# A second tile for the sums of the 1024-feature norms, their statistics traced at top priority, and a reciprocal square root by Ln and Exp in the GLA head norms

## The chip, the cores and the metric

The kernel runs on one core of one Trainium2 chip. The metric is the device time of one execution in microseconds; the time before is the median of three runs. A profile is one further execution of the same program, read by the hardware profiler. Its engines are TensorE (PE in the rows, with its weight loads as PEld), VectorE (DVE), ScalarE (ACT), GpSimd (POOL) and SyncE (SP, which here only issues transfers).

## What is computed

One inference step of a two-layer hybrid backbone over 640 tokens: 128 context tokens and 512 latent tokens, 1024 features each. Layer 0 mixes tokens by a chunked gated linear attention (GLA, four heads of 128 output features) and a multi-head latent attention side by side; layer 1 does differential attention. Each layer ends in a gated MLP of width 2816 with a width-3 convolution. Ahead of each of these four sublayers, and once more at the end, stands an RMS norm over the 1024 features. The GLA heads have a norm of their own.

```python
def rmsnorm(x, g):
    y = xf * lax.rsqrt(jnp.mean(xf * xf, axis=-1, keepdims=True) + EPS)
    return y * g
def modulate(h, shift, scale):
    return h * (1.0 + scale) + shift
...
hp = modulate(rmsnorm(xp, norm_gain[l, 0]), mp[0], mp[1])     # five norms of this width in all
...
o = rmsnorm(o, gla_gain) * jax.nn.silu(ga)                    # GLA: over the 128 features of a head
```

The shift, scale and gate of each sublayer come from a linear map of the SiLU of a conditioning vector.

## The kernel before

Features lie on the 128 partitions, in eight blocks k of 128 features (`x[:, k]`), and tokens along the free dimension. The 640 tokens are worked in two halves of 320 columns (`CH`). Each projection is a set of matmuls in a split precision: a weight tile and an activation tile each have a high part and a low part, and three matmuls of 128x128 by 320 columns make one product; the high parts are casts on ScalarE, the low parts subtractions on VectorE or GpSimd. `B` holds the normed activations in the two parts, and the matmuls of a sublayer walk over its eight blocks k.

The code is traced by a tile framework, whose planner lays out every engine's queue by a simulated timeline before the kernel runs: of the instructions that are ready there, the one traced earliest goes first, and a tile is taken from its pool's ring when its first writer is laid out. After that each engine works through its queue strictly in order. `tc.issue_after(ins)` keeps what a block traces behind `ins` in the queue of the engine of `ins`; it puts nothing on instructions of other engines. In the code before, `Ada.step` nests one such block for a VectorE instruction and one for a transfer.

The norm over 1024 features is `rms` (L227). For one half it squares block 0 on ScalarE into the tile `racc` (L235), squares blocks 1 to 7 into the two tiles `rsq` (L238), and adds each to `racc` on VectorE (L239). A matmul with a matrix of minus ones sums over partitions and spreads the sum (L242, tile `rb`). ScalarE takes Ln (L244) and Exp (L245, written back into `racc`) for a first value of the reciprocal root, squares it (L247), and two VectorE instructions improve it (L248, L250). `racc` has one buffer, so the half that comes second can begin its first square only when L250 of the first half has read that buffer.

`norm_mod` (L321) is this and then `apply_norm` (L303): for each block k, VectorE multiplies `x` by the spread root and the gain (L311, in two pieces where context and latent tokens meet in the first half), ScalarE adds the shift and makes the high part (L313, L177), and VectorE (L315, even k) or GpSimd (L178, odd k) makes the low part. `norm_mod` runs three times for two halves each: ahead of the MLP of layer 0 (about 430 to 470 us of the profile), ahead of layer 1's attention (about 900 to 945 us), ahead of the MLP of layer 1 (about 1305 to 1340 us). Each time the matmuls of an output projection (`out_mm`, tile `pot`, L345) finish half 0 of `x` first and half 1 after, with a residual addition for each block (L327), so half 0 is normed beside the matmuls of half 1. Then the first matmuls of the next sublayer (`up` at L201, or `qko` and `vo` at L216 and L1051) run over half 0 and after that over half 1.

At the start of the kernel both halves are normed from the loaded `x` (L444) beside the four steps `ada0` (L417), which make shift and scale of the first norm on TensorE, each ended by a copy to SBUF on VectorE (L431); blocks 0 to 3 are modulated after the second of them, blocks 4 to 7 after the fourth. There too ScalarE applies Silu to the gate vectors `cbc` (L471), for use in products on VectorE later (L368). The last norm is `final` (L1179): half 0 is finished on GpSimd (L1187, L1188), half 1 on VectorE (L1190) and stored.

The GLA head norms use `rms_stats` (L253): squares (L260), small matmuls that bring the sums of 64 tokens into columns (L266), and then, on a tile of 64 rows by 8, a reciprocal square root on VectorE alone: a seed from two integer operations (L272, L273) and three Newton steps of three instructions (L275 to L277). The GLA works through five chunks of 128 tokens; it calls `stats` for chunks 0 to 2 in its main loop and for chunks 3 and 4 later, beside the first work of the latent attention. The same function serves the differential attention of layer 1.

Of the kernel before, what the change touches and what calls it, by code (L numbers as in the profile page):

```python
# [7 lines left out]
FP32 = mybir.dt.float32  # L8
# [4 lines left out]
I32 = mybir.dt.int32  # L13
ACTF = mybir.ActivationFunctionType
# [5 lines left out]
D = 1024  # L20
# [36 lines left out]
def build(tc, a):  # L57
# [166 lines left out]
        with tc.issue_after(after.ins) if after else ExitStack():  # L224
            mark["tab"] = S.preload_act_table_set("natural_log_exp_and_others")

    def rms(tp, bank, parts, denom, out=None, y=None, after=None):  # L227

        n = parts[0].shape[-1]

        def sq_tile():
            return tp.tile([128, CUT], FP32, tag="rsq", name="rsq", bufs=2)[:, 0:n]

        acc = tp.tile([128, CUT], FP32, tag="racc", name="racc")[:, 0:n]
        S.activation(out=acc, in_=parts[0], func=ACTF.Square)  # L235
        for s in parts[1:]:
            sq = sq_tile()
            S.activation(out=sq, in_=s, func=ACTF.Square)  # L238
            V.tensor_tensor(out=acc, in0=acc, in1=sq, op=ALU.add)  # L239
        o, q, y = bank[:, 0:n], sq_tile(), acc if y is None else y  # L240
        with tc.issue_after(after.ins) if after else ExitStack():
            PE.matmul(out=o, lhsT=negs, rhs=acc, start=True, stop=True)  # L242
        with tc.issue_after(mark["tab"].ins):
            S.activation(out=q, in_=o, func=ACTF.Ln, scale=-1.0 / denom, bias=epst[:, 0:1])  # L244
            S.activation(out=y, in_=q, func=ACTF.Exp, scale=-0.5, bias=lnh[:, 0:1])  # L245
        y = y.bitcast(FP32)
        S.activation(out=q, in_=y, func=ACTF.Square, scale=2.0 / math.sqrt(denom))  # L247
        V.scalar_tensor_tensor(out=o, in0=o, scalar=-denom * EPS, in1=q, op0=ALU.add, op1=ALU.mult)  # L248
        out = o if out is None else out
        V.scalar_tensor_tensor(out=out, in0=o, scalar=3.0, in1=y, op0=ALU.add, op1=ALU.mult)  # L250
        return out

    def rms_stats(tp, bank, srcs, denom):  # L253
        sizes = [s[0].shape[-1] // 64 for s in srcs]
        nb = sum(sizes)
        sums = bank[0:64, 0:2 * nb].rearrange("p (c t) -> p c t", t=2)
        b0 = 0
        for parts, n in zip(srcs, sizes):
            acc = tp.tile([128, CUT], FP32, tag="racc", name="racc")[:, 0:64 * n]
            S.activation(out=acc, in_=parts[0], func=ACTF.Square)  # L260
            for s in parts[1:]:
                sq = tp.tile([128, CUT], FP32, tag="rsq", name="rsq", bufs=2)[:, 0:64 * n]
                S.activation(out=sq, in_=s, func=ACTF.Square)
                mark["acc"] = V.tensor_tensor(out=acc, in0=acc, in1=sq, op=ALU.add)
            for c in range(n):
                PE.matmul(out=sums[:, b0 + c], lhsT=acc[:, c * 64:(c + 1) * 64], rhs=negs[:, 0:2], start=True, stop=True)  # L266
            b0 += n
        y = tp.tile([64, 20], FP32, tag="ry", name="ry")[:, 0:nb]
        v = tp.tile([64, 20], FP32, tag="rv", name="rv")[:, 0:nb]
        t = tp.tile([64, 20], FP32, tag="rt", name="rt")[:, 0:nb]  # L270
        V.tensor_scalar(out=v, in0=sums[:, :, 0], scalar1=-1.0 / denom, scalar2=EPS, op0=ALU.mult, op1=ALU.add)
        V.tensor_scalar(out=t.bitcast(I32), in0=v.bitcast(I32), scalar1=1, scalar2=None, op0=ALU.logical_shift_right)  # L272
        V.tensor_scalar(out=y.bitcast(I32), in0=t.bitcast(I32), scalar1=-1, scalar2=0x5F3759DF, op0=ALU.mult, op1=ALU.add)  # L273
        for _ in range(3):
            V.tensor_tensor(out=t, in0=y, in1=y, op=ALU.mult)  # L275
            V.scalar_tensor_tensor(out=t, in0=t, scalar=-0.5, in1=v, op0=ALU.mult, op1=ALU.mult)
            V.scalar_tensor_tensor(out=y, in0=t, scalar=1.5, in1=y, op0=ALU.add, op1=ALU.mult)  # L277
        return y
# [41 lines left out]

    def norm_mod(tp, bank, x, hl, l, n, half):  # L321
        c0, c1 = CH[half]
        return apply_norm(tp, x, rms(tp, bank, [x[:, k, c0:c1] for k in range(KT)], D), hl, l, n, half)

    def resid(x, k, ps_ap, l, g, c0=0, c1=TOK):
        for s0, s1, c in seg(c0, c1):
# [114 lines left out]
            make_g(0, 0, (g // 2) * 4, (g // 2) * 4 + 4)  # L441

    ada0(0)
    bcs = [rms(xp, ps("s", "rb")[:, 0:512], [x[:, k, c0:c1] for k in range(KT)], D) for c0, c1 in CH]  # L444
    for g in range(1, 4):
        ada0(g)
        if g % 2:
# [20 lines left out]
    adp.after = [last, load]  # L468
    with tc.issue_after(load.ins):
        adp.load(a["cbc"])  # L470
    S.activation(out=adp.cbc, in_=adp.cbc, func=ACTF.Silu)  # L471
    cbd = drp.tile([128, 2, D], FP32, name="cbd")
    nc.gpsimd.dma_start(out=cbd, in_=adp.cbc)
    for c in range(2):
# [228 lines left out]
            S.copy(out=oo[r], in_=op[:, r, 0:256])  # L703

    def stats(c):
        RY[c] = rms_stats(scp, ps("m", "rb"), [[z] for z in OO[c]], 128.0)

    def finish(c):
        oo, y, t0 = OO.pop(c), RY.pop(c), c * 128
# [398 lines left out]
    def diff_after(h, g, q0, n, ops):  # L1108
# [4 lines left out]
        if g == (1 if h == 7 else 2):  # L1113
# [4 lines left out]
                split(o, A[0][:, h], A[1][:, h])  # L1118

            def stats():  # L1120
                y = rms_stats(oo_, ps("p1", "rb"), [[o[:, c0:c1]] for c0, c1 in CH], 128.0)
                later(DLY if h == 6 else 0, lambda: finish(y))

            def later(n, f):
# [54 lines left out]
    def final(c):  # L1179
        c0, c1 = CH[c]  # L1180
        bcs = nm.tile([128, CUT], FP32, tag="bcs", name="bcs") if c == 0 else None
        bc = rms(nm, ps("p1", "rb"), [x[:, k, c0:c1] for k in range(KT)], D, bcs)
        k0 = 0
        for k in range(KT):
            xk, fg = x[:, k, c0:c1], sm["fgain"][:, k:k + 1]
# [174 lines left out]
```

## Time and profile before

| | us |
|---|---|
| median of 3 runs | 1810.37 |
| lowest and highest | 1806.56, 1814.55 |
| the profiled execution | 1809.02 |
| its span, first to last instruction | 1807.2 |

Busy time in that span: TensorE 1740.0 us (96%), VectorE 1263.0 us (70%), ScalarE 759.9 us (42%), GpSimd 312.0 us (17%). The mean granted clock of TensorE is 0.984 of full speed. To read it: TensorE is near to always busy, so what a stage can gain is first the sum of TensorE's pauses there, and then what its clock loses after a pause. Which instruction ended a pause is read from the waits; what that instruction itself stood behind is read from the timelines of the other engines.

### The profile page before, as it was taken

The numbers are of one execution on the slowest core, as the hardware profiler recorded it, in microseconds if no ns is written. First come the engines' busy times: TensorE is split into PE (matmuls) and PEld (weight loads), VectorE is DVE, ScalarE is ACT, GpSimd is POOL, SyncE is SP. The second block draws the span as 40 slices with busy tenths as digits, with TensorE's granted clock in tenths as the row PEclk, the third lists the DMA queues.
The fourth block names the chain that finished last, engine by engine and source line by source line (L and its number), as shares of the span: only waits on it lengthen the run. The fifth ranks groups of instructions, "written<-read, shape, count | busy, mean of one in ns | idle before, by whom it ended". The sixth has DMA issues, their size and how long they took to land. (4 is left out here: it accounts for less than half of the span.)

```text
span 1807.2 us, 29445 instructions
## 1 busy us (share of the span) xinstructions
PE 1740.0 (96%) x11716; PEld 1628.6 (90%) x11716; DVE 1263.0 (70%) x2438; ACT 759.9 (42%) x1344; POOL 312.0 (17%) x330
## 2 busy tenths in 40 slices
PE   7999989999999999999999999999999999999996
PEld 1898777889899999999988999898989999999996
DVE  4964886768699999955588777876575454545556
ACT  5354434544522222322366665665373232323232
POOL 3201021000310100000124233431041010101004
PEclk9999999999999999999999999998999999999998
DMA  9650002035256555522232110211122222222221
GB/s 356 208 177 9 29 1 71 6 141 163 81 170 199 169 186 172 177 61 83 73 116 72 33 58 32 76 49 71 59 72 87 76 71 82 71 82 70 59 83 59
DMA packets 57337, 176.59 MB, mean 98 GB/s; under 512 B 6064, under 2 KB 11568, under 8 KB 56816
## 3 DMA queue, kind: packets, MB, share of 16 engines
q1 hardware_dynamic: 53408, 160.59, 27.8%
q0 software_dynamic: 3792, 14.13, 2.2%
q8 instruction: 92, 1.51, 0.3%
q14 instruction: 45, 0.37, 0.1%
HBM read 166.59 MB, written 7.77 MB: 96 GB/s over the span
## 5 line engine op out<-in xcount | busy, mean ns | idle before, releaser
L207 PE MATMUL up<-B,whi 128*128 128x320 f32 x2560 | 479.2, 309 | 0.0
L163 ACT CAST whi<-wraw 128x1024 fp32r<-128x1024 f32 (+2 forms) x208 | 208.3, 1002 | 505.9 <-PE up L207 231.3
L207 PEld LDWEIGHTS up<-B,whi 128*128 128x128 f32 x2560 | 401.7, 188 | 0.0
L170 DVE TENSOR_TENSOR wlo<-wraw,whi 128x1024 fp32r<-128x1024 f32 (+2 forms) x175 | 205.0, 1172 | 226.2 <-ACT whi L163 226.0
L207 PE MATMUL up<-B,wlo 128*128 128x320 f32 x1280 | 291.5, 309 | 0.0
L207 PE MATMUL po<-A,whi 128*128 128x320 f32 x1312 | 246.2, 309 | 0.7 <-DVE u L972 0.5
L207 PEld LDWEIGHTS up<-B,wlo 128*128 128x128 f32 x1280 | 213.9, 188 | 0.0
L368 DVE CUSTOM_DVE_ANT_0 junk<-araw,cbc 128x1024 bf16<-128x1024 f32 x160 | 203.3, 1271 | 11.1 <-DMA araw<-in_wada0b 8.8
L207 PEld LDWEIGHTS po<-A,whi 128*128 128x128 f32 x1312 | 205.7, 188 | 1.4 <-issue 0.7
L178 POOL TENSOR_TENSOR A<-u,A 128x640 fp32r<-128x640 f32 x44 | 75.8, 1723 | 757.2 <-ACT A L177 732.2
L207 PE MATMUL po<-A,wlo 128*128 128x320 f32 x656 | 149.7, 309 | 0.5 <-DVE wlo L170 0.5
L216 PE MATMUL qko<-B,whi 128*128 128x320 f32 x512 | 119.1, 317 | 2.9 <-ACT B L177 1.5
L170 POOL TENSOR_TENSOR wlo<-wraw,whi 128x256 fp32r<-128x256 f32 (+1 forms) x117 | 97.8, 865 | 134.5 <-ACT whi L163 133.8
L345 PE MATMUL pot<-A,whi 128*128 128x320 f32 x512 | 113.9, 311 | 0.0
L207 PEld LDWEIGHTS po<-A,wlo 128*128 128x128 f32 x656 | 109.6, 188 | 0.8 <-DVE wlo L170 0.8
L970 DVE SCALAR_TENSOR_TENSOR u<-up,small,u 128x127 f32<-128x127 f32 (+1 forms) x176 | 95.4, 542 | 9.0 <-ACT u L968 8.2
L972 DVE SCALAR_TENSOR_TENSOR u<-up,small,u 128x127 f32<-128x127 f32 (+1 forms) x176 | 96.1, 547 | 4.5
L857 ACT ACTIVATE p<-sc,mn 128x768 f32<-128x768 f32 (+1 forms) x100 | 79.2, 796 | 31.9 <-DVE mn L856 31.2
L216 PEld LDWEIGHTS qko<-B,whi 128*128 128x128 f32 x512 | 86.7, 191 | 5.8 <-ACT B L177 2.1
L856 DVE TENSOR_REDUCE mn<-sc 128x1 f32<-128x768 f32 (+1 forms) x100 | 79.2, 815 | 14.6 <-PE sc L831 14.2
L345 PEld LDWEIGHTS pot<-A,whi 128*128 128x128 f32 x512 | 85.7, 188 | 1.1 <-issue 0.4
L207 PE MATMUL pe<-B,whi 128*128 128x320 f32 x416 | 81.5, 318 | 3.1 <-DVE nm_t L311 2.1
(294 smaller groups left out, 3035.4 us busy)
## 6 DMA issues: line engine op xcount, KB each, us to landing
wraw<-in_wup SPq DMA_DIRECT2D x88, 512.0 KB, 3.6
araw<-in_wada SPq DMA_DIRECT2D x48, 512.0 KB, 3.5
wraw<-in_wdn SPq DMA_DIRECT2D x40, 512.0 KB, 3.6
araw<-in_wada0b SPq DMA_DIRECT2D x32, 512.0 KB, 4.3
wraw<-in_wie SPq DMA_DIRECT2D x13, 512.0 KB, 4.4
aw<-in_wada0a SPq DMA_DIRECT2D x8, 512.0 KB, 8.1
wraw<-in_wada0a SPq DMA_DIRECT2D x8, 512.0 KB, 8.0
wraw<-in_woe SPq DMA_DIRECT2D x8, 512.0 KB, 4.3
```

The lines of the kernel that those rows point to most:

```text
L163: S.copy(out=hi, in_=raw)
L170: eng.tensor_tensor(out=lo[:, z], in0=raw[:, z], in1=hi[:, z].bitcast(FP32), op=ALU.subtract)
L178: return (lo_eng or V).tensor_tensor(out=lo, in0=src, in1=hi.bitcast(FP32), op=ALU.subtract)
L207: PE.matmul(out=o, lhsT=w[wi][:, k], rhs=hl[ri][:, k, c0:c1], start=k == 0 and n == 0, stop=k == nk - 1 and n == 2)
L216: PE.matmul(out=o, lhsT=w[wi][:, k], rhs=hl[ri][:, k, c0:c1], start=k == 0 and n == 0, stop=k == nk - 1 and n == 2)
L345: PE.matmul(out=o, lhsT=ws[j + m][wi][:, k], rhs=hl[ri][:, k, c0:c1], start=k == 0 and n == 0, stop=k == nk - 1 and n == 2)
L368: V.tensor_tensor_reduce(out=junk, in0=raw, in1=self.cbc[:, j], op0=ALU.mult, op1=ALU.add, scale=1.0, scalar=0.0, accum_out=mods[l][:, t0 ...
L856: V.tensor_reduce(out=mn[:, m:m + 1], in_=ss[m][:, 0:nk], op=ALU.min, axis=AX.X)
L857: self.exp = S.activation(out=p[:, m, 0:nk], in_=ss[m][:, 0:nk], func=ACTF.Exp, scale=-1.0, bias=mn[:, m:m + 1], accum_out=li[:, m:m + 1])
L970: V.scalar_tensor_tensor(out=u[:, s0 + 1:s1], in0=r[:, s0:s1 - 1], scalar=cw[:, 0:1], in1=u[:, s0 + 1:s1], op0=ALU.mult, op1=ALU.add)
L972: last = V.scalar_tensor_tensor(out=u[:, s0:s1 - 1], in0=r[:, s0 + 1:s1], scalar=cw[:, 2:3], in1=u[:, s0:s1 - 1], op0=ALU.mult, op1=ALU.add)
```

## The change

- `rms` takes the number of buffers of `racc`; the start norm, `norm_mod` and `final` pass 2. The calls with 128 and 256 features keep one.
- In `norm_mod` the call of `rms` is traced inside `tc.high_priority()`, which gives its instructions the priority of the program's start.
- The Silu of `cbc` is traced inside `tc.issue_after(last.ins)`. `last` is what `apply_norm` returned, the VectorE instruction of L315.
- `rms_stats` has a parameter `seed`. Where it is true (the GLA head norms) the two integer operations are replaced by Ln and Exp on ScalarE, queued behind the table load `mark["tab"]`, and one Newton step is made instead of three. The differential attention passes false and stays as it was.

```diff
-    def rms(tp, bank, parts, denom, out=None, y=None, after=None):
+    def rms(tp, bank, parts, denom, out=None, y=None, after=None, bufs=1):
...
-        acc = tp.tile([128, CUT], FP32, tag="racc", name="racc")[:, 0:n]
+        acc = tp.tile([128, CUT], FP32, tag="racc", name="racc", bufs=bufs)[:, 0:n]
...
-    def rms_stats(tp, bank, srcs, denom):
+    def rms_stats(tp, bank, srcs, denom, seed):
...
-        V.tensor_scalar(out=t.bitcast(I32), in0=v.bitcast(I32), scalar1=1, scalar2=None, op0=ALU.logical_shift_right)
-        V.tensor_scalar(out=y.bitcast(I32), in0=t.bitcast(I32), scalar1=-1, scalar2=0x5F3759DF, op0=ALU.mult, op1=ALU.add)
-        for _ in range(3):
+        if seed:
+            with tc.issue_after(mark["tab"].ins):
+                S.activation(out=t, in_=v, func=ACTF.Ln)
+                S.activation(out=y, in_=t, func=ACTF.Exp, scale=-0.5)
+        else:
+            V.tensor_scalar(out=t.bitcast(I32), in0=v.bitcast(I32), scalar1=1, scalar2=None, op0=ALU.logical_shift_right)
+            V.tensor_scalar(out=y.bitcast(I32), in0=t.bitcast(I32), scalar1=-1, scalar2=0x5F3759DF, op0=ALU.mult, op1=ALU.add)
+        for _ in range(1 if seed else 3):
...
     def norm_mod(tp, bank, x, hl, l, n, half):
         c0, c1 = CH[half]
-        return apply_norm(tp, x, rms(tp, bank, [x[:, k, c0:c1] for k in range(KT)], D), hl, l, n, half)
+        with tc.high_priority():
+            bc = rms(tp, bank, [x[:, k, c0:c1] for k in range(KT)], D, bufs=2)
+        return apply_norm(tp, x, bc, hl, l, n, half)
...
-    bcs = [rms(xp, ps("s", "rb")[:, 0:512], [x[:, k, c0:c1] for k in range(KT)], D) for c0, c1 in CH]
+    bcs = [rms(xp, ps("s", "rb")[:, 0:512], [x[:, k, c0:c1] for k in range(KT)], D, bufs=2) for c0, c1 in CH]
...
-    S.activation(out=adp.cbc, in_=adp.cbc, func=ACTF.Silu)
+    with tc.issue_after(last.ins):
+        S.activation(out=adp.cbc, in_=adp.cbc, func=ACTF.Silu)
...
-        RY[c] = rms_stats(scp, ps("m", "rb"), [[z] for z in OO[c]], 128.0)
+        RY[c] = rms_stats(scp, ps("m", "rb"), [[z] for z in OO[c]], 128.0, True)
...
-        bc = rms(nm, ps("p1", "rb"), [x[:, k, c0:c1] for k in range(KT)], D, bcs)
+        bc = rms(nm, ps("p1", "rb"), [x[:, k, c0:c1] for k in range(KT)], D, bcs, bufs=2)
```

## Rows read from the trace of the kernel before

**Rows 1.** The page: its head, and the first line of its part on busy time (busy us, share of the span, instructions).

```profile
span 1807.2 us, 29445 instructions
...
PE 1740.0 (96%) x11716; PEld 1628.6 (90%) x11716; DVE 1263.0 (70%) x2438; ACT 759.9 (42%) x1344; POOL 312.0 (17%) x330
```

**Rows 2.** The waits of TensorE over the whole span: its instruction, the engine and line that ended the pause, the pauses' sum in us, their number, the longest.

```profile
PE up L201 <- ACT B L313: 6.3, 2, 3.2
...
PE rb L242 <- DVE racc L239: 4.2, 1, 4.2
...
PE pe L207 <- DVE nm_t L311: 2.1, 1, 2.1
...
PE up L201 <- DVE B L315: 1.9, 2, 1.0
...
PE qko L216 <- ACT B L177: 1.5, 1, 1.5
...
PE gp L666 <- DVE ry L277: 1.2, 2, 1.0
```

**Rows 3.** VectorE's timeline from 1278 to 1340 us, the norm ahead of the MLP of layer 1 (start, duration in us, line, operation, tiles, count, and in brackets the idle time before and what ended it).

```profile
1307.80 0.55 DVE L327 SCALAR_TENSOR_TENSOR x2t<-pot,mod,x2t 128x320 f32<-128x320 f32 x1 [1.77 <-PE pot L345]
...
1312.46 0.49 DVE L250 SCALAR_TENSOR_TENSOR rb<-rb,racc 128x320 f32<-128x320 f32 x1
...
1320.54 0.54 DVE L327 SCALAR_TENSOR_TENSOR x2t<-pot,mod,x2t 128x320 f32<-128x320 f32 x1
...
1327.63 1.08 DVE L239 TENSOR_TENSOR racc<-racc,rsq 128x320 f32<-128x320 f32 x2
1332.02 0.50 DVE L248 SCALAR_TENSOR_TENSOR rb<-rb,rsq 128x320 f32<-128x320 f32 x1 [3.31 <-ACT rsq L247]
...
1333.17 1.47 DVE L311 SCALAR_TENSOR_TENSOR nm_t<-x2t,gs,rb 128x320 f32<-128x320 f32 x3
```

**Rows 4.** ScalarE's timeline of the same stretch.

```profile
1313.03 0.46 ACT L235 ACTIVATE racc<-x2t 128x320 f32<-128x320 f32 x1
...
1330.37 0.53 ACT L244 ACTIVATE rsq<-rb,scal 128x320 f32<-128x320 f32 x1 [1.98 <-PE rb L242]
```

**Rows 5.** Five stretches of the span: from and to, length, busy us (and instructions) of PE, PEld, DVE, ACT and POOL, then the granted clock of TensorE as a share of full speed, the busy share of the DMA engines and GB/s. The first lies in the first projection, the second behind the GLA, the third at the MLP of layer 0 (behind a pause), the fourth at layer 1's attention, the fifth at the MLP of layer 1 (behind a pause).

```profile
55.00:58.00 3.00, 3.00 (x12) 3.00 (x13) 2.77 (x6) 2.57 (x6) 1.56 (x2) 0.50 0.52 173
304.00:308.00 4.00, 3.72 (x15) 2.71 (x14) 1.46 (x3) 2.11 (x5) 2.32 (x4) 0.50 0.22 41
462.10:466.00 3.90, 3.62 (x21) 3.09 (x22) 3.64 (x8) 3.52 (x8) 2.05 (x2) 1.00 0.00 2
925.30:928.60 3.30, 3.30 (x13) 3.14 (x14) 3.30 (x10) 2.61 (x8) 1.38 (x1) 0.52 0.54 159
1335.00:1338.00 3.00, 3.00 (x13) 2.85 (x12) 2.75 (x6) 2.66 (x6) 2.04 (x2) 0.50 0.00 0
```

**Rows 6.** The timeline of all engines from 1786.9 to 1800 us, the last norm.

```profile
1787.85 0.47 ACT L235 ACTIVATE racc<-x2t 128x320 f32<-128x320 f32 x1
1787.97 8.39 POOL L1188 TENSOR_TENSOR x2t<-x2t,bcs 128x320 f32<-128x320 f32 x8 [5.54 <-DVE bcs L250]
...
1791.17 0.31 PE L345 MATMUL pot<-A,wlo 128*128 128x320 f32 x1
...
1792.37 0.54 DVE L327 SCALAR_TENSOR_TENSOR x2t<-pot,mod,x2t 128x320 f32<-128x320 f32 x1
...
1792.83 2.81 DVE L239 TENSOR_TENSOR racc<-racc,rsq 128x320 f32<-128x320 f32 x3
...
1795.70 1.44 PE L242 MATMUL rb<-racc,negs 128*128 128x320 f32 x2 [4.22 <-DVE racc L239]
```

**Rows 7.** VectorE's groups of instructions from 165 to 310 us, the GLA and the first work behind it, shapes kept apart: busy us and mean ns of one, then idle time before them.

```profile
L277 DVE SCALAR_TENSOR_TENSOR ry<-rt,ry 64x8 f32<-64x8 f32 x15 | 2.9, 190 | 0.3
...
L275 DVE TENSOR_TENSOR rt<-ry 64x8 f32<-64x8 f32 x15 | 2.3, 154 | 0.3
...
L276 DVE SCALAR_TENSOR_TENSOR rt<-rt,rv 64x8 f32<-64x8 f32 x15 | 2.2, 150 | 0.2
...
L272 DVE TENSOR_SCALAR rt<-rv 64x8 int32<-64x8 int32 x5 | 1.3, 267 | 0.1
...
L273 DVE TENSOR_SCALAR ry<-rt 64x8 int32<-64x8 int32 x5 | 0.8, 158 | 0.1
```

**Rows 8.** ScalarE's groups of the same stretch: the smallest ACTIVATE, an Exp on 128 rows by 2.

```profile
L726 ACT ACTIVATE scal<-scal 128x2 f32<-128x2 f32 x1 | 0.2, 198 | 0.0
```

**Rows 9.** The timeline of all engines from 296 to 306 us: the head norm of the last chunk, from its first small operation to the matmul that needs the result.

```profile
298.42 0.16 DVE L271 TENSOR_SCALAR rv<-rb 64x8 f32<-64x8 f32 x1 [0.31 <-PE rb L266]
...
302.04 0.70 PE L287 MATMUL rbc<-rdg,negs 64*128 64x256 f32 x2 [0.74 <-DVE rdg L283]
```

**Rows 10.** The timeline of all engines from 24 to 42 us, the norm at the start.

```profile
31.80 0.49 DVE L239 TENSOR_TENSOR racc<-racc,rsq 128x320 f32<-128x320 f32 x1
...
36.77 0.81 PE L242 MATMUL rb<-racc,negs 128*128 128x320 f32 x2
...
38.03 0.67 DVE L431 COPY ar<-adaps 4x512 f32<-4x512 f32 x1
...
40.54 1.47 DVE L311 SCALAR_TENSOR_TENSOR nm_t<-x0t,gs,rb 128x320 f32<-128x320 f32 x3
...
40.71 1.91 ACT L471 ACTIVATE cbc<-cbc 128x2048 f32<-128x2048 f32 x1
```

More of the change, by code (lines that the diff above doesn't have):

```diff
@@ L1120, in stats @@
             def stats():
-                y = rms_stats(oo_, ps("p1", "rb"), [[o[:, c0:c1]] for c0, c1 in CH], 128.0)
+                y = rms_stats(oo_, ps("p1", "rb"), [[o[:, c0:c1]] for c0, c1 in CH], 128.0, False)
                 later(DLY if h == 6 else 0, lambda: finish(y))
```

## The prediction

> **What bounds the kernel now.** I read the page first, then TensorE's waits, then the other engines' timelines around each wait, then the clock. TensorE is busy 1740.0 of 1807.2 us [rows 1], so at most some 67 us are pauses, and an edit elsewhere pays only where it shortens one. The waits name those that end on a norm [rows 2]: two of 3.2 us for the first high part of half 1 ahead of an MLP, one of 4.2 us at the end, 2.1 us in the first projection, two of about 1 us for a low part of half 0, 1.5 us at layer 1's attention, 1.2 us behind the small operations of the GLA norms. Some pauses cost again afterwards: behind those at 55, 304, 925 and 1335 us TensorE ran at a granted clock of about 0.50 (its 1.2 GHz level) for 3 to 4 us, but not behind the equal pause at 462 us, where it stayed at 1.00, the 2.4 GHz level [rows 5]. At half clock half the time is lost, 1.5 us in the fifth row. I work from the profiled execution, 1809.0 us (span 1807.2 and 1.8 around it); the median of the runs is 1.4 above it, inside their scatter.
>
> **The norm ahead of layer 1's MLP (second tile and priority together).** Half 1's first square starts at 1313.03 [rows 4], just after half 0's L250 has read the one tile (1312.46 and 0.49) [rows 3], though four blocks of x have long been ready. From there VectorE has no pause until its last addition ends at 1327.63 + 1.08 = 1328.71; then the chain of matmul, Ln, Exp, square and L248 leaves it idle for 3.31 us, and half 1's first L311 starts at 1333.17 [rows 3]. With two tiles and top priority the seven additions follow the residuals. Those of blocks 1 to 4 fit into pauses such as the 1.77 us at 1307.80 [rows 3]; that takes 4 x 0.48 = 1.9 us out of the full stretch (0.48 is my figure from 1.08 us for a pair, which overlap a little). The last follows the residual of 1320.54 [rows 3], so the chain of some 4.5 us (1328.71 to 1333.17) runs beside half 0's multiplications and puts 1.0 us (L248, L250) into the stretch. VectorE then reaches half 1's L311 at 1328.71 - 1.9 + 1.0 = 1327.8 instead of 1333.17, its high part is there 1.2 us later at 1329.0 (as 1333.17 to the start of TensorE at 1334.4), and TensorE has half-0 work until 1334.4 - 3.2 = 1331.2. The 3.2 us wait goes, with 2 us in hand; next late is half 0 itself, whose 1 us wait stays or grows. I count 2.8 for the wait and 1.5 for the half clock [rows 5]: **4.3 us**. Bounds: 5.7 with the 1 us wait gone too; a loss of 1.5 if half 0's parts are late by more than is saved.
>
> **The norm ahead of layer 0's MLP.** The same waits, of the same length [rows 2], but without the half clock [rows 5]: **2.8 us**, from -1.5 to 4.1.
>
> **The norm ahead of layer 1's attention.** Here half 1 makes no pause, because enough half-0 work covers it; the 1.5 us wait is for half 0, block 1 [rows 2], followed by half clock at 925 us (1.7 us lost) [rows 5]. Additions of blocks 1 to 3 leave the full stretch (1.5 us back), but L248, L250 and the last three additions move in ahead of half 0's parts (2.5 us). Between a gain of 3.2 and a loss of 4 I take **0**.
>
> **The last norm (second tile alone).** Half 1's first square stands at 1787.85 behind half 0's release [rows 6]; the additions then queue up, and even the residual of the last block waits for them, to 1792.37, though TensorE finished it at 1791.17 + 0.31 = 1791.48 [rows 6]. With its own tile only the last residual (0.54), square (0.47) and addition are left after 1791.48: 1793.0 to 1793.5, against 1792.83 + 2.81 = 1795.64. That is 2.1 to 2.6 us; I take 2.3. The matmul behind it took 1.44 us after its pause of 4.22 [rows 6]; with the pause halved I add 0.5. **2.8 us**, from 1.0 to 3.4. The three additions there took 0.94 us each beside GpSimd's multiplications, against 0.48 elsewhere [rows 3, 6]. The Trainium skill, "SBUF — State Buffer", Who interferes with whom, says that a VectorE instruction with two SBUF inputs and a GpSimd instruction that reads SBUF exclude each other for the whole instruction; by it the last addition can wait out one GpSimd multiplication (8.39 / 8 = 1.05 us), and the tail would give 1.7 instead of 2.3.
>
> **The start (second tile alone).** Half 1's last addition is at 31.80, its matmul at 36.77, its first L311 at 40.54 [rows 10]. Its chain can now run beside half 0's, up to 6 us sooner, which empties VectorE before blocks 4 to 7 come; TensorE's 2.1 us wait names L311 there, and half clock follows it [rows 2, 5]. Against it: half 1's multiplications (1.47 for three, so about 2 for four) and two low parts (about 1) would now be ready ahead of the copy of 38.03 [rows 10], which ends an `ada0` step and lets TensorE's next one begin. So from -3.2 to 2.1 + 1.5 = 3.6; nearer the wait that names L311, I take **1.5 us**.
>
> **Silu.** The block names a VectorE instruction, the Silu is ScalarE's, and the construct ties only instructions of one engine. So it holds nothing, and the Silu (1.91 us) [rows 10] goes where the planner puts it. Were it held, only products that TensorE doesn't wait for would start later. Nothing either way.
>
> **GLA seeds.** Eight VectorE instructions of each call go: 0.267 + 0.158 + 2 x (0.190 + 0.154 + 0.150) = 1.41 us [rows 7]. Two on ScalarE come, about 0.2 each by the nearest row [rows 8], both on the chain, so 1.0 net. In the main loop TensorE waits 1.2 us by name for the last of these operations [rows 2], more for copies queued among them; for three chunks I take 0.5 each, 1.5. The last chunk runs bare: 298.42 to 302.04, with a wait of 0.74 at its end [rows 9], of which 0.7 goes. The half clock behind it (2 us lost in four) [rows 5] may go; I count 0.8. **3.0 us**, from -2.5 (below) to 5.
>
> **Sum.** 4.3 + 2.8 + 0 + 2.8 + 1.5 + 0 + 3.0 = 14.4 us, 0.8%. 1809.0 - 14.4 = 1794.6.
>
> **The rivals.** (a) The pause moves to half 0. Seven additions and two multiplications at top priority stand ahead of half 0's parts, TensorE's waits of about 1 us grow to about 3, and the half clock stays. For it: VectorE has no pause in that stretch, and L311 and L315 are what it is short of. Against it: four of the additions find pauses earlier. MLPs 1 us each, attention -1, start 0, GLA 2, end 2.8: 1803. The Trainium skill, "TensorE: Matmul & The Clock Gate", Part 1, has the clock follow how busy the engine has lately been; by it a pause that only changes place would keep its half clock. The rows agree on four stretches and not on the one at 462 us [rows 5]. (b) ScalarE is the new wait in the GLA: Ln and Exp queue between the exponentials on which matmuls and products wait, 0.5 us a chunk, -2.5 instead of 3.0, which gives 1800. For it, every call makes two more changes of engine; against it, ScalarE is mostly idle there. (c) **Slower.** The chain itself, with its idle 3.31 us, is queued on VectorE ahead of half 0's multiplications instead of beside them. Half 0's parts are then late by 3.3 + 1.0 + 1.5 = 5.8 us at each of the three norms. The MLPs lose 5.8 - 3.2 = 2.6 each, with another 1.5 at half clock in the first; the attention, which saves nothing, 5.8: 12.5 lost, against 6 gained elsewhere, 1815. It decides as soon as over 3.2 us of idle time on VectorE lie ahead of half 0's L311; against it, the planner fills a queue with what is ready. (d) That the change doesn't do what it says holds for the Silu alone, and its price is nothing.
>
> **How the numbers follow.** My forecast has 0.59, (a) 0.21, (b) 0.12, (c) 0.08. The forecast's own range, with its bounds, is 1784 to 1803. The range reaches to (a) and (b) and the upper part of their scatter: 1782 to 1808; (c) and the outer ends are left out. About 0.5% (9 us, below 1801 or above 1819) is what a measurement of this kernel can tell from no change. Below 1801: 0.53 of the forecast, 0.07 of (b), 0.04 of (a), together 0.64. Above 1819: only the far half of (c) and a queue that comes out badly elsewhere, 0.05. The rest is 0.31.
>
> **What would show it.** Half 1's squares of blocks 0 to 3 before half 0's L250; VectorE without an idle 3 us ahead of L248; no 3 us wait of `up` on L313, and full clock behind it; the last L242 less than 2.5 us after the last `pot`; three small Newton operations a chunk; no table load between Ln and Exp. I am wrong if waits of `up` or `qko` on half 0's L315, L177 or L178 grow by 2 us and more, if the copy of L431 moves later than 38 us, or if waits on ScalarE grow in the GLA.

## The result and the profile after

The changed kernel takes 1789.24 us (median of 4 runs, 1787.32 to 1795.88) against 1810.3 us (median of 4 runs of the kernel before): the ratio is 0.9893, with a 95% interval from 0.9871 to 0.9914. The forecast was 1794.6, in a range from 1782 to 1808, faster. The profiled run took 1789.83 us, with a span of 1788.1, 19.1 us less than before [rows 1].

The page of the changed kernel, its head and TensorE's line:

```profile
span 1788.1 us, 29411 instructions
...
PE 1730.6 (97%) x11716; PEld 1622.1 (91%) x11716; DVE 1256.9 (70%) x2398; ACT 757.4 (42%) x1354; POOL 310.0 (17%) x330
```

The waits of TensorE in the changed kernel (columns as in [rows 2]; from line 272 on its lines are shifted by 5 to 8, so L318 is L313 of before, L316 is L311, L839 is L831):

```profile
PE rb L242 <- DVE racc L239: 3.2, 1, 3.2
...
PE up L201 <- POOL B L178: 2.2, 4, 0.9
PE pe L207 <- DVE nm_t L316: 2.1, 1, 2.1
...
PE qko L216 <- ACT B L318: 1.6, 1, 1.6
...
PE qko L216 <- ACT B L177: 1.3, 1, 1.3
...
PE qko L216 <- POOL B L178: 1.2, 1, 1.2
...
PE gp L674 <- DVE ry L282: 0.5, 1, 0.5
```

The two waits of `up` for half 1's first high part, 6.3 us together [rows 2], are gone; what is left of `up` waits for a low part, 2.2 us in all and 0.9 at the longest, where it was 2.1 and 1.0. The last wait went from 4.2 to 3.2 only. The first projection's 2.1 us is unchanged, and the attention norm has waits of 1.6, 1.3 and 1.2 us where its longest was 1.5 [rows 2].

**Where the 19.1 us came from.** Both kernels run the same 11,716 matmuls, so the start of the same matmul in each trace says how much had been gained up to there. The table takes the 616th into `pe`, the 111th into `pot`, the 102nd into `up`, the 119th into `qko`, the 565th into `pot`, the 2250th into `up`, and the end of the span; in the trace of before they start at 152.3, 433.8, 467.3, 955.6, 1316.9 and 1345.7, and the span is 1807.2. Each column is the gain within its stretch (us; minus is a loss), for one profiled execution of each kernel ("forecast" has the terms of the sum):

| kernel | to 152 | GLA, to 434 | MLP norm, layer 0 | attention norm, layer 1 | to 1317 | MLP norm, layer 1 | last norm | sum |
|---|---|---|---|---|---|---|---|---|
| forecast | 1.5 | 3.0 | 2.8 | 0 | | 4.3 | 2.8 | 14.4 |
| changed kernel | 2.6 | 7.1 | 2.8 | -0.2 | 1.8 | 3.5 | 1.5 | 19.1 |
| e6, the same again | 2.6 | 7.3 | 2.8 | -0.3 | 1.8 | 3.5 | 1.5 | 19.2 |
| e1, seeds alone | 1.6 | 7.2 | -1.0 | 0.1 | 1.7 | 0.1 | -0.1 | 9.6 |
| e2, all but seeds | -0.6 | 0.4 | 2.8 | -0.1 | 0.6 | 3.5 | 1.0 | 7.4 |
| e3, tiles alone | 3.2 | 1.6 | 2.8 | 2.0 | -1.0 | 3.5 | 1.1 | 13.2 |
| e4, priority alone | 0.4 | -4.0 | -1.1 | 0.4 | -2.4 | 0.1 | 0.0 | -6.6 |
| e5, tiles and seeds | 4.0 | 7.2 | 2.8 | 1.1 | -6.0 | 3.5 | 1.4 | 13.9 |
| e7, no GpSimd in the tail | 2.3 | 5.6 | 2.8 | -0.2 | -2.3 | 3.5 | 2.6 | 14.2 |
| e8, one Newton step | 1.0 | 6.5 | -0.9 | 0.1 | -1.5 | 0.3 | -0.1 | 5.5 |
| e9, Silu held | -2.0 | 6.8 | 2.7 | -0.2 | -3.4 | 3.5 | 1.0 | 8.4 |
| e10, tail on VectorE | 2.0 | 7.2 | 2.8 | 0.6 | 1.7 | 3.5 | 0.0 | 17.8 |
| e11, no priority in attention | 2.0 | 7.2 | 2.8 | 0.9 | -2.9 | 3.5 | 1.4 | 14.8 |
| e12, Silu held, tail on VectorE | -3.6 | 7.1 | 2.8 | -0.2 | 0.5 | 3.5 | 0.0 | 10.1 |

**The MLP norm of layer 1.** VectorE and then ScalarE in the changed kernel (columns as in [rows 3] and [rows 4]):

```profile
1297.50 0.50 DVE L248 SCALAR_TENSOR_TENSOR rb<-rb,rsq 128x320 f32<-128x320 f32 x1 [0.46 <-ACT rsq L247]
...
1298.76 0.49 DVE L250 SCALAR_TENSOR_TENSOR rb<-rb,racc 128x320 f32<-128x320 f32 x1
...
1310.69 0.48 DVE L239 TENSOR_TENSOR racc<-racc,rsq 128x320 f32<-128x320 f32 x1
...
1315.18 0.50 DVE L248 SCALAR_TENSOR_TENSOR rb<-rb,rsq 128x320 f32<-128x320 f32 x1 [1.03 <-ACT rsq L247]
...
1316.33 1.47 DVE L316 SCALAR_TENSOR_TENSOR nm_t<-x2t,gs,rb 128x320 f32<-128x320 f32 x3
```

```profile
1268.18 0.83 ACT L235 ACTIVATE racc<-x2t 128x320 f32<-128x320 f32 x2
...
1312.83 0.53 ACT L244 ACTIVATE rsq<-rb,scal 128x320 f32<-128x320 f32 x1 [0.64 <-PE rb L242]
```

Both halves' first squares stand next to each other at 1268.18, 30 us ahead of half 0's L250 at 1298.76; before, the second one came behind that L250 [rows 3, 4]. The idle time of VectorE ahead of half 1's L248 has shrunk from 3.31 us [rows 3] to 1.03.

**The clock.** The stretches of [rows 5] in the changed kernel, in the same order (one in the first projection, behind the GLA, at both MLP norms and at layer 1's attention), with the columns of that group:

```profile
48.00:51.00 3.00, 3.00 (x13) 3.00 (x13) 2.96 (x8) 2.56 (x7) 0.22 (x1) 0.54 0.57 183
294.00:298.00 4.00, 3.71 (x26) 3.01 (x24) 1.92 (x6) 1.42 (x4) 2.30 (x3) 1.00 0.00 0
449.60:453.50 3.90, 3.62 (x22) 3.09 (x22) 3.63 (x8) 3.52 (x8) 2.04 (x2) 1.00 0.00 0
915.00:918.00 3.00, 3.00 (x15) 3.00 (x14) 3.00 (x9) 1.82 (x5) 0.23 (x1) 0.54 0.64 199
...
1317.50:1320.50 3.00, 2.72 (x16) 2.16 (x16) 2.74 (x6) 2.81 (x6) 1.60 (x2) 1.00 0.00 0
```

The second and the last were at 0.50 before and are at full clock now; 26 matmuls fall into the four us behind the GLA, where there were 15.

**The last GLA chunk** in the changed kernel, VectorE, ScalarE and TensorE (columns as in [rows 9]):

```profile
290.35 0.15 DVE L271 TENSOR_SCALAR rv<-rb 64x8 f32<-64x8 f32 x1
...
291.12 0.21 ACT L274 ACTIVATE rt<-rv 64x8 f32<-64x8 f32 x1
...
291.36 0.21 ACT L275 ACTIVATE ry<-rt 64x8 f32<-64x8 f32 x1
...
291.60 0.16 DVE L280 TENSOR_TENSOR rt<-ry 64x8 f32<-64x8 f32 x1
...
292.18 0.42 DVE L288 TENSOR_TENSOR rdg<-nid,ry 64x256 f32<-64x256 f32 x1
...
293.01 0.70 PE L292 MATMUL rbc<-rdg,negs 64*128 64x256 f32 x2
```

No table load stands between Ln and Exp, three Newton operations are left, and the matmul no longer waits: other matmuls fill the time in front of it. From L271 to the operation that makes `rdg` it is 1.83 us, where it was 3.15 (298.42 [rows 9] to 301.57).

**The last norm** in the changed kernel (columns as in [rows 6]):

```profile
1770.66 7.90 POOL L1196 TENSOR_TENSOR x2t<-x2t,bcs 128x320 f32<-128x320 f32 x8 [5.80 <-DVE bcs L250]
...
1770.89 2.10 DVE L239 TENSOR_TENSOR racc<-racc,rsq 128x320 f32<-128x320 f32 x2
...
1773.37 1.77 DVE L239 TENSOR_TENSOR racc<-racc,rsq 128x320 f32<-128x320 f32 x2
...
1773.59 0.31 PE L352 MATMUL pot<-A,wlo 128*128 128x320 f32 x1
1775.07 0.54 DVE L334 SCALAR_TENSOR_TENSOR x2t<-pot,mod,x2t 128x320 f32<-128x320 f32 x1
...
1776.20 0.82 DVE L239 TENSOR_TENSOR racc<-racc,rsq 128x320 f32<-128x320 f32 x1 [0.59 <-ACT rsq L238]
...
1777.08 0.81 PE L242 MATMUL rb<-racc,negs 128*128 128x320 f32 x2 [3.18 <-DVE racc L239]
```

TensorE is done with the last block at 1773.59 + 0.31 = 1773.90, and the residual that needs it starts at 1775.07: two additions of 0.89 us each, beside GpSimd's multiplications, stand ahead of it.

### The profile page after: what moved, and what is told of

Same layout as the page of the kernel before. It is cut to its first block, busy times and chain, and to the rows that moved or that the text cites. A ratio compares the mean times of both kernels' runs of the same rounds, so it can differ in the third digit from the quotient of the medians.

```text
span 1788.1 us, 29411 instructions
## 1 busy us (share of the span) xinstructions
PE 1730.6 (97%) x11716; PEld 1622.1 (91%) x11716; DVE 1256.9 (70%) x2398; ACT 757.4 (42%) x1354; POOL 310.0 (17%) x330
## 5 line engine op out<-in xcount | busy, mean ns | idle before, releaser
L375 DVE CUSTOM_DVE_ANT_0 junk<-araw,cbc 128x1024 bf16<-128x1024 f32 x160 | 204.6, 1279 | 10.2 <-DMA araw<-in_wada0b 8.2
L864 DVE TENSOR_REDUCE mn<-sc 128x1 f32<-128x768 f32 (+1 forms) x100 | 79.2, 816 | 13.7 <-PE sc L839 13.4
L334 DVE SCALAR_TENSOR_TENSOR x2t<-po,mod,x2t 128x128 f32<-128x128 f32 x88 | 44.2, 546 | 55.3 <-PE po L207 50.6
```

What stands on the lines that cost most here:

```text
L375: V.tensor_tensor_reduce(out=junk, in0=raw, in1=self.cbc[:, j], op0=ALU.mult, op1=ALU.add, scale=1.0, scalar=0.0, accum_out=mods[l][:, t0 ...
L864: V.tensor_reduce(out=mn[:, m:m + 1], in_=ss[m][:, 0:nk], op=ALU.min, axis=AX.X)
```

## The experiments

Each was compared with runs of the kernel before on its own chip (medians 1811.98 for e1 to e4, 1808.08 for e5 to e8, 1809.18 for e9 to e12).

**e1, the seeds alone; e2, everything but the seeds.** e1 is the kernel before with the lines of `rms_stats` and its two calls from the diff; e2 is the changed kernel without them. The Silu is not tied in e1 to e4.

> The kernel before with the change's GLA seeds alone (Ln and Exp, one Newton step), all large norms as before. Theory S (each part earns its own stage; what the GLA gained, 7.2 us between 211 and 311 us of the trace, comes from the seeds, about half of it as the half-clock stretch behind the last chunk that disappears): the span is 6.5 to 8.5 us shorter than before, no stretch at a granted clock of 0.5 between 300 and 312 us, the three late waits (3.2, 3.2 and 4.2 us) stay. Rival R (the seeds bring only the 3.0 us of the forecast or less, the rest of the GLA's gain is an order of the queues that came with the other edits): span 1 to 4 us shorter, and the half-clock stretch near 304 us stays.

> The changed kernel without the seeds: second tiles everywhere and the priority, GLA norms as before. Theory S: the GLA loses its gain, everything else stays, so the span is 11 to 13 us shorter than before (start 1.9, first MLP norm 2.8, attention 1.4 by a shorter half-clock stretch at 966 us, second MLP norm 3.5, tail 1.5) and half clock shows again near 304 us. Rival R: part of the GLA's gain is here, span 14 us or more shorter than before.

e1: 1801.71 us, ratio 0.9948 (0.9928 to 0.9968), span 1797.6. The GLA gains 7.2 us, as in the changed kernel, at full clock behind it, and the late waits are still there: Theory S. That its span fell by 9.6 us, more than the expected 8.5, lies in the start and in the stretch up to 1317. e2: 1798.54 us, ratio 0.9931 (0.9911 to 0.9950), span 1799.8. Its GLA gains 0.4 and runs at half clock again behind the last chunk, while both MLP norms gain the changed kernel's 2.8 and 3.5. The gain of the span, 7.4, fell short of the 11 to 13 us by some 4, most of it in the start and in the stretch up to 1317, which the seeds don't touch. More half clock lay in the start (13.7 us of it in the first 61 us instead of 6.8), but e7 had as much there and still gained, so this is not shown to be the cause. The profiled executions were also not typical: e1's was the shortest of its six and e2's the longest. By the medians the two are 10.3 and 13.4 us below the kernel before, both somewhat more than Theory S asks for. The stretch behind e2's GLA, columns as in [rows 5]:

```profile
303.00:307.00 4.00, 3.10 (x10) 1.88 (x9) 1.28 (x3) 0.41 (x1) 2.27 (x3) 0.50 0.00 0
```

e1 showed something more. Its MLP norm of layer 0 is that of before, to the operation, and the pause there is as long as before [rows 2]. But in e1 half clock follows it, in the trace of before it didn't [rows 5]. TensorE's first matmul behind the pause, and the stretch behind it:

```profile
453.30 1.20 PE L201 MATMUL up<-B,whi 128*128 128x320 f32 x4 [3.15 <-ACT B L318]
```

```profile
455.00:458.00 3.00, 3.00 (x14) 3.00 (x13) 2.75 (x6) 2.70 (x6) 2.12 (x3) 0.53 0.00 0
```

**e3, the second tile without priority; e4, priority without the second tile.**

```
e3:      bc = rms(tp, bank, [...], D, bufs=2)          # also at the start and the last norm
e4:      with tc.high_priority():
             bc = rms(tp, bank, [...], D, bufs=1)
```

> The kernel before with second tiles for the sums in all 1024-feature norms, but no priority for the norms ahead of the MLPs and the attention. Theory P (the second tile is what frees half 1's squares; the priority only orders what is ready): start and tail as in the changed kernel, both MLP norms gain at least 2 us, waits for half 1's first high part under 1.5 us. Rival Q (without priority the planner still puts half 1's additions behind half 0's multiplications, so the tile alone does little): both 3.2 us waits stay above 2 us, span 3 to 5 us shorter than before from start and tail alone.

> The kernel before with the priority alone, one tile for the sums. Theory P: half 1's first square still has to wait for half 0's last use of the one tile, so both 3.2 us waits stay (2.5 to 3.5 us), span within 2 us of before. Rival Q: the priority is what moves the work, the waits fall below 1.5 us. A loss is possible on either side if the top-priority chain now stands ahead of half 0's multiplications with its idle 3.3 us: span 2 to 8 us longer.

e3: 1796.6 us, ratio 0.9911 (0.9886 to 0.9936), span 1794.0. Both MLP norms gain 2.8 and 3.5 us without any priority, to 0.1 us what the changed kernel gains. e4: 1809.87 us, ratio 0.9997 (0.9981 to 1.0013): no change; the two 3.2 us waits stand as before. So Theory P holds, and at the MLP norms the priority adds nothing. e4's profiled run, the longest of its twelve, was 6.6 us longer than before, and 4.0 of them lie in the GLA, whose instructions it doesn't touch: a half-clock stretch of 10 us that the other runs don't have there. At layer 1's attention the tile alone gained 2.0 us, where with the priority 0.2 is lost.

**e5, tile and seeds without priority; e11, priority taken from attention alone.**

```
e5:      bc = rms(tp, bank, [...], D, bufs=2)
e11:     with ExitStack() if n == 0 else tc.high_priority():
             bc = rms(tp, bank, [...], D, bufs=2)
```

> The changed kernel without the priority: second tiles and seeds. Theory P (tile and seeds carry everything; the priority only takes VectorE away from half 0's parts at layer 1's attention, where the kernel with tiles alone gained some 4 us more than the one with tiles and priority): 1783 to 1787 us, 2 to 5 us below the changed kernel, no 1.8 us wait of sc near 952 us, MLP norms as in the changed kernel. Rival Q (the priority adds something once the seeds are in): 1788 us or more.

> The changed kernel with the priority taken from layer 1's attention norm alone; the norms ahead of the MLPs keep it. Theory A (in the run without any priority all of the 5 us were lost behind this norm, in the softmax of the first heads and in half clock there, none at the MLPs): the same loss here, 1793 to 1797 us, a wait of ptp for the difference of maps of about 3.4 us near 984 us. Rival M (the MLP norms' priority mattered for the order further on): 1788 to 1791 us.

e5: 1795.77 us, ratio 0.9929 (0.9906 to 0.9952); the expected 1783 to 1787 was wrong. The attention norm did gain (1.1 against -0.2), but 6.0 us are lost behind it. The wait that does it is in the maps of the first heads; e5's TensorE there, with the idle time in brackets:

```profile
973.03 0.87 PE L881 MATMUL ptp<-small,p 128*128 128x128 f32 x6 [3.41 <-DVE p L1111]
```

The stretch from 975 to 985 us behind it ran at a granted clock of 0.72 on average, that from 1055 to 1065 at 0.66. In the changed kernel the waits in the same stage are shorter, the longest 1.82 us, for `sc`. e11: 1794.38 us, ratio 0.9918 (0.9901 to 0.9935), with the same 3.4 us wait of `ptp`: Theory A. So with the seeds in, the priority at the attention norm is worth some 5 us (on e5's chip e6, the changed kernel again, took 1790.03 us), not by shortening a wait there, but by the order in which the work behind it comes out. Without the seeds it is worth nothing: on one chip e2, with the priority, took 1798.54 us and e3, without it, 1796.6, and e3 doesn't have this wait of `ptp`. It takes both the seeds and the missing priority to make the wait, and why the order comes out so was not followed up.

**e6, the changed kernel again.**

> The changed kernel once more, unaltered. It shows what one profile can be off by: if the half-clock stretches are tied to pauses alone they stand where they stood (30, 48, 914, 955, 1044, 1232 and 1263 us of the trace, none near 304 and none near 440 and 1323); if they come and go by themselves, at least one of the seven moves, and the start differs by 1 us or more. Span 1786 to 1794 us.

1790.03 us, ratio 0.9901 (0.9878 to 0.9923). Every column agrees with the first profile to 0.2 us, the half-clock stretches stand where they stood, and the start differs by 0.05 us. So a trace of the same kernel repeats itself here, clock and all; yet of this kernel's runs one took 1796.12, and one of the first four 1795.88, which neither profile shows.

**e7, the last norm without GpSimd.** `G.tensor_tensor(out=xk, in0=xk, in1=bcs, op=ALU.mult)` is left out (one run).

> The changed kernel with GpSimd's eight multiplications of half 0 by the broadcast norm left out (half 0 of the result is then not normed). Theory C (they slow VectorE's additions beside them, 0.82 to 1.05 us instead of 0.48, so the last residual queues and the last wait is 3.2 instead of about 2 us): the additions of the last norm take 0.48 to 0.50 us, the last wait of rb is 1.9 to 2.4 us. Rival T (the tail is the chain of residual, square, addition and semaphores, whatever GpSimd does): the wait stays at 3.0 to 3.3 us.

VectorE and TensorE at the end of e7 (columns as in [rows 6]):

```profile
1779.35 0.49 DVE L239 TENSOR_TENSOR racc<-racc,rsq 128x320 f32<-128x320 f32 x1 [0.20 <-ACT rsq L238]
1779.96 0.55 DVE L334 SCALAR_TENSOR_TENSOR x2t<-pot,mod,x2t 128x320 f32<-128x320 f32 x1
...
1781.10 0.49 DVE L239 TENSOR_TENSOR racc<-racc,rsq 128x320 f32<-128x320 f32 x1 [0.60 <-ACT rsq L238]
...
1781.65 0.81 PE L242 MATMUL rb<-racc,negs 128*128 128x320 f32 x2 [1.73 <-DVE racc L239]
```

The additions take 0.48 to 0.49 us, the residual starts as soon as its block is there, and the wait is 1.73 us: Theory C. The tail gains 2.6 instead of 1.5. Everything ahead of the tail is the changed kernel's own program, and yet the start, the GLA and the stretch to 1317 gained 0.3, 1.5 and 4.1 us less than there. The clock of e7, and then of the changed kernel, in two places of the same work:

```profile
214.00:217.00 3.00, 3.00 (x13) 2.73 (x12) 2.67 (x6) 0.55 (x2) 0.00 (x0) 0.50 0.02 5
1057.00:1063.00 6.00, 6.00 (x22) 5.37 (x22) 5.80 (x13) 4.12 (x9) 0.33 (x1) 0.50 0.30 89
```

```profile
213.50:216.50 3.00, 3.00 (x24) 2.55 (x22) 2.74 (x6) 2.03 (x6) 0.00 (x0) 1.00 0.02 5
1054.00:1060.00 6.00, 6.00 (x38) 5.28 (x38) 6.00 (x12) 3.71 (x10) 1.94 (x3) 1.00 0.30 90
```

**e8, integer seeds with one Newton step.** In the kernel before, the loop of L274 runs once instead of three times for the GLA's norms.

> The kernel before with integer seeds and one Newton step instead of three in the GLA norms (less exact; six small VectorE instructions fewer in each call, nothing on ScalarE). Theory L (what pays in the GLA is that fewer VectorE instructions stand between the sums and the matmul; where the seed comes from doesn't matter): the GLA, 211 to 311 us, is 6 to 9 us shorter, no half clock near 304 us, the waits on L283 and on ry, rt fall below 1.5 us together. Rival E (the move to ScalarE is what pays): less than 3 us.

1803.48 us, span 1801.7 (one run). The GLA gains 6.5 us, runs at full clock behind the last chunk, and its waits on `rdg`, `ry` and `rt` are 0.8 us together, where they were 4.8: Theory L. What pays is that fewer small instructions stand in a row on VectorE; that the seed comes from ScalarE makes no more than the 0.7 us between 6.5 and 7.2, by one profile each. The clock behind e8's GLA:

```profile
302.00:306.00 4.00, 3.38 (x23) 2.95 (x22) 3.71 (x10) 3.05 (x7) 0.81 (x1) 1.00 0.96 388
```

**e9, the Silu really held; e10, the last multiplications on VectorE; e12, both.**

```
e9:   mark["mod"] = S.activation(out=u if k % 2 else hi[:, r], in_=u, ...)   # L318
      with tc.issue_after(mark["mod"].ins):                                 # instead of last.ins
          S.activation(out=adp.cbc, in_=adp.cbc, func=ACTF.Silu)
e10:  half 0: V.scalar_tensor_tensor(out=xk, in0=xk, scalar=fg, in1=bcf[0], ...)
      behind rms of half 1, no GpSimd
```

> The changed kernel with the gate vector's Silu tied to a ScalarE instruction, the last L318 of the first norm, so that it is held. Theory N (as forecast: only products follow it that TensorE doesn't wait for): the Silu moves from 40.9 to 53 to 58 us, half 1's first L318 comes 1.4 us sooner, at 41.3, and TensorE's work at 100 us stands within 0.7 us of where the changed kernel has it. Rival G (its table load and itself, 3.2 us on ScalarE, are what half 1 of the first norm waits for): TensorE is 1 to 3 us ahead at 100 us and the 2.1 us wait for nm_t is shorter than 1 us. Rival H (the products start late and VectorE is late for the weight splits behind them): 1 us or more behind at 125 us.

> The changed kernel with half 0's eight last multiplications on VectorE, written behind half 1's sums, instead of sixteen instructions on GpSimd. Theory C (GpSimd's multiplications stretched the additions): additions of 0.48 to 0.50 us, the last wait of rb 1.7 to 2.2 us, the end 1 to 2 us sooner; all eight multiplications (0.47 us each) fit into VectorE's pauses before the last chain. Rival V (they queue ahead of the last residual or push half 1's multiplications back): the wait is 3 us or more, or the end no sooner. Median 1787 to 1789 us by C.

> The changed kernel with both: the Silu held on ScalarE and half 0's last multiplications on VectorE. If the two add up with what each gave alone by Theory C and Rival G: 1784 to 1788 us; by Theory C and N: 1787 to 1790 us. A different set of half-clock stretches in the middle, as the run without GpSimd's tail showed on the same code, can put it 3 to 6 us above either.

e9: 1800.61 us (one run). The Silu goes from 40.91 to 56.19, and half 1's first L318 comes 2.15 us behind L247 instead of 3.60, so 1.4 sooner. So Rival G is right in part: at the 60th matmul into `pe` e9 was 5.0 us ahead of the changed kernel, some of it from before the Silu, and at 100 us still 0.9, though its wait for `nm_t` is still 1.7. But the products that use the Silu (L375, 1.23 us each on VectorE), which begin at 58.1 us in place of 58.3, wait longer for the transfers of their weights (12.0 us in all instead of 7.4) and are done at 123.1 instead of 117.7. One of them, at 119.03, and a weight split stand in front of the GLA's `ab` (L528, at 121.32 instead of 118.80), for which TensorE waits; half clock follows:

```profile
122.06 1.44 PE L207 MATMUL pe<-B,whi 128*128 128x320 f32 x4 [2.93 <-DVE ab L528]
```

```profile
121.50:127.00 5.50, 4.94 (x18) 4.95 (x19) 5.50 (x8) 3.10 (x4) 2.69 (x2) 0.50 0.40 123
```

By 152 us it has lost 2.0 where the changed kernel has gained 2.6: Rival H by its number, though the products did not start later; why their transfers did was not followed up. e10: 1790.04 us, ratio 0.9893 (0.9871 to 0.9914), no better than the changed kernel's 1789.24 and 1790.03. The additions are 0.48 to 0.56 us now, but VectorE does all eight multiplications at one go:

```profile
1771.11 3.78 DVE L1198 SCALAR_TENSOR_TENSOR x2t<-x2t,small,bcs 128x320 f32<-128x320 f32 x8
...
1774.81 0.48 DVE L239 TENSOR_TENSOR racc<-racc,rsq 128x320 f32<-128x320 f32 x1
...
1777.85 1.43 PE L242 MATMUL rb<-racc,negs 128*128 128x320 f32 x2 [4.13 <-DVE racc L239]
```

The last two residuals queue behind them, and the wait for the last sum is 4.13 us: Rival V. e12: 1796.83 us, ratio 0.9932 (0.9915 to 0.9950): both losses together. No version here beats the changed kernel.

## Why the forecast came out as it did

The direction and the range were right; two terms of the sum were mis-sized, the GLA's last chunk and the last norm, and they partly cancel. By the table the sum is 4.7 us too small: 4.1 in the GLA, 1.1 in the start and 1.8 in the stretch up to 1317, for which it had no term, against 1.3 too much for the last norm, 0.8 for the MLP norm of layer 1 and 0.2 for the attention.

**MLP norms: right in the mechanism.** 2.8 was forecast for layer 0 and 2.8 measured; 4.3 for layer 1 and 3.5 measured, the wait and its half clock gone. Half 1's first L316 came at 1316.33, which is 1330.4 on the old scale (14.1 us had been gained by then), not 1327.8. The 2 us in hand were not there: the first high part of half 1 was done at 1317.47 and the matmul that reads it began at 1317.53, right behind half 0's. ScalarE and TensorE in the changed kernel:

```profile
1316.91 0.56 ACT L318 ACTIVATE B<-nm_t,mod 128x320 fp32r<-128x320 f32 x1 [1.42 <-DVE nm_t L316]
...
1317.53 1.20 PE L201 MATMUL up<-B,whi 128*128 128x320 f32 x4
```

So the wait went with next to nothing to spare. The priority, which I counted with the tile, does nothing here (e3, e4). Rival (a) and rival (c) fell: half 0's waits did not grow (2.1 us before, 2.2 after), and the chain is not queued ahead of half 0 as an idle stretch. Two slips of the working changed nothing: 0.48 us for an addition is right, but the pair of 1.08 us from which I took it gives 0.54; and in rival (c) the terms gained elsewhere are 2.8 + 1.5 + 3.0 = 7.3 us, not 6.

**GLA: the mechanism right, the term of the last chunk too small.** Up to the 93rd matmul into `op`, at 271.6 us of the old trace, 1.9 us were gained, where I had 1.5 for the main loop. The rest, over 5 us, came from the last chunk, for which I had 0.7 of one wait and 0.8 of the half clock. The wait of [rows 9] went, and the next one of the kernel before:

```profile
303.64 1.04 PE L287 MATMUL rbc<-rdg,negs 64*128 64x256 f32 x2 [0.90 <-DVE rdg L283]
```

Matmuls of the next stage now fill the place. With the waits went all of the half clock from 303.9 to 310.7, where half the time was lost, 3.4 us. The ten traces with a short chain have none there (the changed kernel, e1, e5 to e12), the four with the long one do (before, e2, e3, e4). Rival (b), a new wait on ScalarE, fell with e1 and e8.

**The last norm: too large by 1.3.** The step that failed: after the last matmul only residual, square and addition are left, 1.5 to 2.0 us. In e7 that is what it takes (1779.92 to 1781.59, 1.7 us). In the changed kernel it took 3.1, because GpSimd's multiplications still lie beside half 1's additions (they begin 3.2 us ahead of the end of the last block, 3.5 before) and stretch those ahead of the last residual to 0.89 to 1.05 us and the last one to 0.82. I had seen 0.94 for these in the trace of before, kept it out of the sum, and priced it beside the sum for one addition only. The wait shrank by 4.22 - 3.18 = 1.04 where I had 2.3, so my sign of less than 2.5 us between the last `pot` and L242 did not come. The 0.5 for the matmul behind the wait was right: 0.81 us instead of 1.44. The Trainium skill, "SBUF — State Buffer", Who interferes with whom, pointed that way, and e7 bears it out; the 1.7 that I made of it was still too much, since the queue of several stretched additions counts, not the last one alone.

**The start: the size about right, the reason wrong.** Half 1's chain did not move: its matmul came at 37.13 and its first L316 at 40.69, within 0.4 us of before [rows 10], and the 2.1 us wait stayed. The additions were done earlier, but the matmul stands in TensorE's queue behind those of L430, which ended at 37.20. What moved is VectorE: half 0's multiplications start at 30.23 (32.20 before), and the copy of L438 stands at 37.24 with idle time in front of it instead of queueing to 38.03 [rows 10]. VectorE in the changed kernel:

```profile
30.23 1.84 DVE L316 SCALAR_TENSOR_TENSOR nm_t<-x0t,gs,rb 128x128 f32<-128x128 f32 x6
...
37.24 0.68 DVE L438 COPY ar<-adaps 4x512 f32<-4x512 f32 x1 [1.33 <-PE adaps L430]
```

Up to the 60th matmul into `pe`, at 61.4 us of before, the traces with one tile (before, e1, e4, e8) gained 0, 0.9, 0.3 and 0.4 us; those with two and a Silu that isn't held 1.3 to 3.2, but e2 lost 1.4. By the means, 0.4 and 1.6, about 1.2 us is the tile's, with more scatter than that between the traces, so the tile's share of the start is not shown. Another 0.7 comes near 122 us; e1 and e8 have it too, e3 hardly (0.2), so it belongs to the order that came out and not to the tile.

**Attention: right as to the norm, for a poor reason.** -0.2 against 0. The gain of 1.8 up to 1317 is a half-clock stretch near 966 us that is half as long, and e1, with the old norm, has it as well. That the order behind this norm decides over 5 us (e5, e11) I had not considered.

**Silu: right that it holds nothing.** It runs at 40.91 (40.71 before [rows 10]). Wrong that holding it would cost nothing, since a matmul of TensorE's does wait behind the products: up to 152 us e9 is 4.6 us and e12 6.2 us behind the changed kernel.

## What to carry to other kernels

A second tile for an accumulator lets two halves' statistics overlap, and that alone brought the whole gain at the MLP norms; a priority on top should be tried by itself, with the other edits in, since its effect may lie far behind the place where it is written. A chain of small operations costs most where it runs bare, at the end of a stage: price it with the half clock behind it. Where an edit frees a chain on one engine, look at which instructions of its neighbours still lie beside it: at the last norm these were GpSimd's multiplications, and moving them to VectorE (e10) cost what it saved.

## What the runs showed of the hardware

**Half clock is not fixed by the pause ahead of it.** The pause of 3.15 to 3.17 us at layer 0's MLP norm was followed by full clock in the trace of before and by half clock in e1, e4 and e8, with the same instructions ahead of it and behind it. The Trainium skill, "TensorE: Matmul & The Clock Gate", Part 1, has the clock follow how busy the engine has lately been; the length of one pause, the only thing I had put in, does not tell it here. Where a whole trace repeats to 0.2 us (e6), the stretches repeat too; in e7, whose start differs by 0.3 us, other stretches appear, worth some 6 us on the same program. So the stage gains of one profile repeated to 0.2 us where the clock agreed, and differed by up to 4 us where it didn't.

**An addition beside GpSimd.** At the start of the changed kernel a 128x320 addition was issued 0.33 us behind one of GpSimd's subtractions and lasted until after it:

```profile
25.56 2.35 POOL L170 TENSOR_TENSOR wlo<-wraw,whi 128x1024 fp32r<-128x1024 f32 x1 [2.89 <-ACT whi L163]
...
25.89 2.37 DVE L239 TENSOR_TENSOR racc<-racc,rsq 128x320 f32<-128x320 f32 x1 [0.45 <-ACT rsq L238]
```

Alone it takes 0.48 us, so it waited out nearly all of GpSimd's 2.35. The Trainium skill's page "SBUF — State Buffer", Who interferes with whom, has VectorE's second SBUF input and GpSimd's reads share one interface; the trace agrees.
